# A layer-input gate from seven products of half blocks, and one joint decode series for gate and up

## The chip, the cores and the metric

The kernel runs on one core of a Trainium2 chip. The metric is the time of one execution on the device, in microseconds (us). Five engines work beside each other, each through its own queue in order: TensorE (PE; its weight loads are shown as PEld), VectorE (DVE), ScalarE (ACT), GpSimd (POOL) and SyncE (SP), which here issues the DMAs. SBUF is the working memory, PSUM holds what TensorE writes.

## The reference

One layer of a streaming encoder: 1024 prompt tokens and 8 x 16 new ("decode") tokens, width 1024, all in float32.

```python
x = x + mix @ w_out                      # attention, not touched here
h = rmsnorm(x, g_ffn)
x = x + (jax.nn.silu(h @ w_gate) * (h @ w_up)) @ w_down     # width 2816
gate = jax.nn.sigmoid(rmsnorm(x, g_ple) @ w_ple_gate)       # 1024 x 1024
x = x + gate * (p @ w_ple_proj)
y = rmsnorm(x, g_final)
```

The tokens make nine tiles of 128 rows: prompt tiles 0 to 7 and the decode tile, number 8 (`NP`).

## The kernel before, in words

Every float32 matrix product is made of three products of rounded parts: an operand is split into `hi` (ScalarE's copy, rounded) and `lo` (the rest, a subtraction by `sub`, line 110), and `mm3` (lines 105 to 108) adds hi x hi, hi x lo and lo x hi in one PSUM bank. `Chunks` (line 125) holds the weights: `raw` loads 1 MB into the only buffer `wraw`, `parts` splits it into a pair of tiles `whi`, `wlo`, of which there are two pairs in turn. A pair comes from `pair` (line 138), which takes two tiles of a rotating tag.

The order of the work is set by a planner, which puts each engine's instructions in order by its own idea of their durations, the program's order deciding between those that are ready. Inside `manual_schedule` blocks the named engines keep the program's order.

*The gate and up projections (loop at line 1144).* Chunk i of 22 holds 256 columns of `w_gate` (even i) or `w_up` (odd i). For the 1024 prompt tokens a chunk's product is made by seven products of half blocks in place of eight (`product`, line 1052: 12 matmuls of 512 columns each, recorded at line 1056): B11, B21, T1 to T4 and B22 are forms of the tokens, quarters of the chunk's weights and their sums S1, S2, S0, S3 are the other side. `sums` (line 1074) makes the weights' sums on VectorE, `sum_parts` (line 1084) splits them on ScalarE and GpSimd, `gate_up_parts` splits the next chunk's weights. `first` makes the first product and copies it from its bank to `u2`, after which the second product is added in the same bank. The 128 decode tokens take the plain way: `decoded` (line 1060), a series of 24 matmuls of 256 columns in each chunk, into bank `e`; a gate chunk's `e` goes through the sigmoid to `dec8` (lines 1169 to 1172), an up chunk's is multiplied onto it. At the end of an up chunk `turned` transposes `dec8` and sends the activations to memory.

*The down projection (loop at line 1335).* Five stages d of 512 of the 2816 rows, again by seven products (`times`, recorded at line 1307; `onto`, line 1312, adds a bank to the residual `x1`; `forms`, line 1275, splits the forms). What all the tokens' first quarter has in common with others is kept in `u2`, four tiles. A last step, `down` (line 1409), does the remaining 256 rows plainly, tile by tile: per tile and half of the columns six matmuls of 512 columns, and, for 12 of the 16 prompt halves, the addition of `u2` on GpSimd (line 1414).

*The layer-input gate (line 1425 to the end).* Behind each tile's last step, `normed` scales its row by the root mean square and by the row `g_ple` (line 199), eight transposes (line 1452) and splits make its transposed parts `hV`. `gate(c, w, t)` (line 1428) makes 256 of the 1024 columns for one tile: 24 matmuls of 256 columns, sigmoid (line 1436), times `proj` (line 1437, loaded by the piece), added to `x1` (line 1438, GpSimd, VectorE for the last c), squared with its sum (line 1439). Four c by nine tiles. The final normalization follows in pieces (lines 1474 to 1483).

## Time and profile before

| | |
|---|---|
| runs | 1726.93, 1732.53, 1733.93 us; median 1732.53 |
| profiled execution | 1727.71 us, its span 1725.6 |
| granted TensorE clock, mean | 0.995 |
| DMA, whole span | 279.40 MB, mean 162 GB/s |
| the gate and up loop | about 880 to 1345 us of the span |
| the down stages | about 1345 to 1580 |
| last step of down, transposes, layer-input gate | about 1573 to 1717.8 |

The profile is of one execution. Times in it count from the start of the span. A busy time is the union of an engine's instructions; matmuls overlap one another, so that a busy TensorE says that it has work, not how fast. An idle time is put down to the last of the semaphores for which the instruction waited. "L1056" is line 1056 of the kernel.

### The profile page before, as it was taken

To read this page: it belongs to the slowest core of one execution; us is meant where nothing else is said; L and a number is where in the kernel's file an instruction comes from. 1 tells how busy PE (TensorE), PEld (TensorE's weight loads), DVE (VectorE), ACT (ScalarE), POOL (GpSimd) and SP (SyncE) were. 2 spreads that over 40 slices of the span, in tenths; PEclk is the share of its full clock that TensorE was granted. 3 is DMA by queue.
4 is the path that set the end of the run, shared out by engine and by line. 5 is a ranking of instruction groups with operands and counts; after the bars stand their busy time and mean duration, and the time that the engine had idled before them with its cause. 6 is when DMAs were issued, how large, how long until landed. Compare 5 with 4: busy or idle time off the path is not lost.

```text
span 1725.6 us, 29066 instructions
## 1 busy us (share of the span) xinstructions
PE 1668.2 (97%) x11076; PEld 1457.6 (84%) x11076; DVE 1044.9 (61%) x1640; ACT 776.4 (45%) x1698; POOL 774.3 (45%) x584
## 2 busy tenths in 40 slices
PE   8999999999997998899999999999999999999998
PEld 7998888889995887787778888888888788887998
DVE  5112344277778675654886666666666698887635
ACT  5214545276767776643643333333332343333432
POOL 2313301287446422222455555555554565558364
PEclk9999999999999999999999999999999999999999
DMA  5847898656469986855413222222222874311123
GB/s 191 278 145 226 287 293 284 189 171 184 119 176 267 296 252 185 232 165 176 142 56 115 88 87 90 95 95 95 95 95 95 291 292 136 120 39 61 59 71 141
DMA packets 172620, 279.40 MB, mean 162 GB/s; under 512 B 15297, under 2 KB 103617, under 8 KB 171074
## 3 DMA queue, kind: packets, MB, share of 16 engines
q1 hardware_dynamic: 172482, 277.55, 49.9%
q8 instruction: 88, 1.44, 0.4%
q14 instruction: 50, 0.41, 0.1%
HBM read 197.95 MB, written 79.56 MB: 161 GB/s over the span
## 4 chain that ended last, share of the span: by engine, by line
PE 86%; DMA 5%; DVE 3%; ACT 2%; issue 1%; POOL 1%; SPq 0%; POOLq 0%; ACTq 0%; DVEq 0%
PE ps L1056 20%; PE ps L106 9%; PE ps L107 9%; PE ps L108 9%; PE pt L1307 6%; PE ps L1307 4%; PE pt L1056 3%; PE pt L608 3%; PE pt L395 2%; PE po L632 2%; DMA mixn<-mixp 2%; PE acc L463 2%; PE po L631 2%; PE S L575 1%; PE sdec L418 1%; PE S L576 1%
## 5 line engine op out<-in xcount | busy, mean ns | idle before, releaser
L111 POOL TENSOR_TENSOR wlo<-wraw,whi 128x512 fp32r<-128x512 f32 (+1 forms) x127 | 224.4, 1794 | 205.6 <-ACT whi L150 201.7
L106 PE MATMUL ps<-whi,hTh 128*128 128x256 f32 x576 | 167.7, 291 | 0.1
L107 PE MATMUL ps<-wlo,hTh 128*128 128x256 f32 x576 | 164.2, 285 | 0.0
L108 PE MATMUL ps<-whi,hTl 128*128 128x256 f32 x576 | 163.9, 285 | 0.0
L150 ACT CAST whi<-wraw 128x512 fp32r<-128x512 f32 (+1 forms) x128 | 88.2, 753 | 94.1 <-PE ps L1056 64.8
L589 DVE TENSOR_TENSOR_SCAN keep<-keep,zero 128x128 f32<-128x128 f32 (+4 forms) x64 | 99.1, 1558 | 37.6 <-ACT keep L581 36.6
L590 POOL TENSOR_TENSOR w<-w,keep 128x127 f32<-128x127 f32 (+4 forms) x64 | 83.4, 1313 | 73.1 <-DVE keep L589 64.0
L106 PEld LDWEIGHTS ps<-whi,hTh 128*128 128x128 f32 x576 | 110.2, 191 | 6.0 <-issue 5.4
L108 PEld LDWEIGHTS ps<-whi,hTl 128*128 128x128 f32 x576 | 110.2, 191 | 0.5 <-DVE hTl L111 0.2
L107 PEld LDWEIGHTS ps<-wlo,hTh 128*128 128x128 f32 x576 | 110.3, 192 | 0.1
L111 DVE TENSOR_TENSOR wtl<-pt,wth 128x512 fp32r<-128x512 f32 (+1 forms) x192 | 94.2, 514 | 18.1 <-ACT wth L612 17.2
L612 ACT CAST wth<-pt 128x512 fp32r<-128x512 f32 (+1 forms) x192 | 84.4, 463 | 44.2 <-PE pt L608 43.4
L608 PE MATMUL pt<-ident,w 128*128 128x128 f32 x528 | 87.9, 278 | 5.5 <-POOL w L590 2.1
L106 PE MATMUL ps<-whi,hVh 128*128 128x256 f32 x288 | 81.9, 284 | 0.5 <-ACT hVh L1454 0.5
L107 PE MATMUL ps<-wlo,hVh 128*128 128x256 f32 x288 | 81.7, 284 | 0.0
L108 PE MATMUL ps<-whi,hVl 128*128 128x256 f32 x288 | 81.6, 284 | 0.0
L575 PE MATMUL S<-qk 128*128 128x384 f32 (+2 forms) x192 | 71.4, 373 | 5.8 <-ACT keep L581 3.9
L631 PE MATMUL po<-wth,vk 128*128 128x256 f32 (+1 forms) x304 | 76.3, 283 | 0.2
L608 PEld LDWEIGHTS pt<-ident,w 128*128 128x128 f32 x528 | 61.8, 141 | 15.4 <-issue 3.6
L632 PE MATMUL po<-wtl,vk 128*128 128x256 f32 (+1 forms) x304 | 72.7, 282 | 0.0
L111 POOL TENSOR_TENSOR actl<-actr,acth 128x1024 fp32r<-128x1024 f32 (+1 forms) x22 | 56.7, 2579 | 33.6 <-DMA sr<-acts 18.2
L106 PE MATMUL ps<-hTh,whi 128*128 128x384 f32 x192 | 66.0, 344 | 0.0
(359 smaller groups left out, 5335.9 us busy)
## 6 DMA issues: line engine op xcount, KB each, us to landing
draw<-in_cache_sb_k SPq DMA_DIRECT2D x32, 512.0 KB, 5.3
draw<-in_cache_sb_v SPq DMA_DIRECT2D x32, 512.0 KB, 5.1
act<-sg SPq DMA_DIRECT2D x11, 1152.0 KB
actr<-act SPq DMA_DIRECT2D x22, 576.0 KB, 5.4
wraw<-in_w_in SPq DMA_DIRECT2D x11, 1024.0 KB, 5.2
wraw<-in_w_gate SPq DMA_DIRECT2D x11, 1024.0 KB
wraw<-in_w_up SPq DMA_DIRECT2D x11, 1024.0 KB
v<-sv SPq DMA_DIRECT2D x36, 256.0 KB, 4.5
```

What stands on the lines that cost most here:

```text
L106: T.matmul(out, lhsT=ah, rhs=bh, start=start, stop=False)
L107: T.matmul(out, lhsT=ah, rhs=bl, start=False, stop=False)
L108: T.matmul(out, lhsT=al, rhs=bh, start=False, stop=stop)
L111: eng.tensor_tensor(out, a, hi.bitcast(F32), op=ALU.subtract)
L150: A.copy(h[:, o], v[:, o])
L575: T.matmul(sc, lhsT=hd["qq"][:, qs], rhs=hd["kkh"][:, kc], start=True, stop=False)
L589: V.tensor_tensor_scan(rev, rev, zero[:, 0:1].to_broadcast([P, n]), 1.0, op0=ALU.mult, op1=ALU.add)
L608: T.transpose(pt[:, (c - c0) * P : (c - c0 + 1) * P], w[:, c * P : (c + 1) * P], ident)
L631: T.matmul(dst, lhsT=vs, rhs=wth[:, kb - base, c0:c1], start=(i == 0), stop=False)
L632: T.matmul(dst, lhsT=vs, rhs=wtl[:, kb - base, c0:c1], start=False, stop=(i == nkb - 1))
L1056: T.matmul(out, lhsT=a[x][:, k], rhs=b[y][:, k], start=(not more and k == 0 and n == 0), stop=(k == 3 and n == 2), skip_group_check=more)
L1307: T.matmul(out, lhsT=a[i][:, x, m * P : (m + 1) * P], rhs=b[j][:, x], start=(not more and x == 0 and n == 0), stop=(x == 1 and n == 2), sk ...
```

## The change

Two parts, and what they need.

*The layer-input gate.* Prompt tiles p and p + 4 make a pair, p from 0 to 3. Of their transposed normalized rows, A11 and A12 are tile p's two halves of the 1024 inputs, A21 and A22 tile p + 4's. With S1 = A21 + A22, S2 = S1 - A11, S3 = A11 - A21, S4 = A12 - S2 and four forms of the weights, seven products of 12 matmuls of 512 columns give both tiles' 1024 columns. The weights' forms are B11, B21, T2 = B22 - (B12 - B11), T3 = B22 - B12, T1 = B12 - B11, B21 - T2 and B22; `g_ple` is multiplied onto the weights' rows, no longer onto the tokens. They are made in `gate_sums(k)` during down stages 1 to 4 (four scalings on ScalarE, four operations on GpSimd, four loads and seven stores of 256 KB each) and stored in `gated`; when the down stages' buffers are free, six are loaded back as 1 MB each into `W` and the seventh, B22, into `wraw`. `weights_parts` splits them: W0, W2, W4 and W6 on ScalarE and VectorE, W1, W3, W5 on ScalarE and GpSimd. The decode tile's outputs are sums over B11 and B21 (24 matmuls of 512 columns) and, for the right half, over B11, T1 and B22 (twice 36 of 256).

The `x1 += u2` additions on GpSimd move ahead of the last down step, whose tiles now go in the order 0, 4, 1, 5, 2, 6, 3, 7, 8. From there on TensorE keeps the program's order. Pair p + 1 is prepared (squares, scaling, transposes, sums, splits) between the products of pair p, and pair 0 in the last down step.

*The decode tokens of gate and up.* The two pairs of weight parts become two places of one `hi` and one `lo` tile, so that one matmul can read both: chunks 0 and 1 keep their own series; from then on a gate chunk has none, and the up chunk behind it makes one series of 24 matmuls of 512 columns for both. `issue_after` puts the splits of the next chunk's weights, on ScalarE and GpSimd, behind the split of the last chunk's sum S0. In the qkv projection one line sets which place is next, since places no longer rotate by themselves.

The diff, cut to its core:

```diff
         def pair(self, k, n):
-            out = []
-            for part in ("hi", "lo"):
-                t_ = self.pool.tile([P, self.width], F32R, name=self.pre + part, tag=self.pre + part, bufs=self.pairs)
-                out.append(t_[:, : k * n].rearrange("p (k n) -> p k n", k=k))
-            return out
+            if self.both is None:
+                self.both = [self.pool.tile([P, self.pairs, self.width], F32R, name=self.pre + part) for part in ("hi", "lo")]
+            self.turn = (self.turn + 1) % self.pairs
+            return [t_[:, self.turn, : k * n].rearrange("p (k n) -> p k n", k=k) for t_ in self.both]
...
             if i:
                 a, u2 = first(w)
+            if i == 1:
                 e = decoded(w, tbank(256))
+            elif up:
+                wts, place = ch.pairs_of(KT)
+                both = tbank().rearrange("p (s n) -> p s n", s=2)
+                for k in range(KT):
+                    mm3(both, h8[0][:, k], h8[1][:, k], wts[0][:, :, k], wts[1][:, :, k], k == 0, k == KT - 1)
+                e0, e = both[:, 1 - place], both[:, place]
             if more and i:
                 raw = gate_up(i + 1)
-                nxt = gate_up_parts(raw)
+                with tc.issue_after(made[0]), tc.issue_after(made[1]):
+                    nxt = gate_up_parts(raw)
...
-            if not up:
+            if i == 0 or up and i > 1:
+                g8 = e if i == 0 else e0
                 t8 = p4b.tile([P, 256], F32, name="t8", tag="t8", bufs=1)
-                A.activation(t8, e, AF.Sigmoid)
-                V.tensor_tensor(dec8, t8, e, op=ALU.mult)
-            else:
+                A.activation(t8, g8, AF.Sigmoid)
+                V.tensor_tensor(dec8, t8, g8, op=ALU.mult)
+            if up:
                 V.tensor_tensor(dec8, dec8, e, op=ALU.mult)
...
+    def gate_sums(k):
+        q = {}
+        for x in range(2):
+            for y in range(2):
+                q[x, y] = wq.tile([P, 512], F32, name=f"q{x}{y}", tag=f"q{x}{y}", bufs=1)
+                row = (x * 4 + k) * P
+                nc.sync.dma_start(q[x, y], w_ple_gate[0, row : row + P, y * 512 : y * 512 + 512])
+                A.activation(q[x, y], q[x, y], AF.Copy, scale=g_gate[:, x * 4 + k : x * 4 + k + 1])
...
+        G.tensor_tensor(t3, q[1, 1], q[0, 1], op=ALU.subtract)
+        G.tensor_tensor(q[0, 1], q[0, 1], q[0, 0], op=ALU.subtract)
+        G.tensor_tensor(t2, q[1, 1], q[0, 1], op=ALU.subtract)
+        G.tensor_tensor(q[1, 0], q[1, 0], t2, op=ALU.subtract)
...
+    W = [own_place(i) for i in range(5)] + [ch.pair(4, 512)]
+    for i in range(6):
+        nc.sync.dma_start(W[i][1].bitcast(F32), gated[i])
+    b22 = ch.raw(gated[6], 4, 512)
...
+    final.enter_context(tc.manual_schedule(engines={mybir.EngineType.PE}))
+    weights_parts(0, V)
+    weights_parts(2, V)
+    for i, t in enumerate(tiles):
+        down(t, w_d, act)
+        if i == 1:
+            coming = prepare(0)
+            next(coming)
+            with tc.issue_after(pows[0].ins):
+                weights_parts(1, G)
+        if i == 4:
+            next(coming)
+            weights_parts(3, G)
+            weights_parts(5, G)
+        if i == 6:
+            forms_ = next(coming)
+            with tc.issue_after(last_split[0]):
+                weights_parts(4, V)
+    W.append(ch.parts(b22, 4, 512, 2, V))
+    fetch_proj((0, 4))
+
+    for p in range(4):
+        A11, A12, S2, S3, S1, A22, S4 = forms_
+        u, u3, u4 = u2[3 * (p % 2)], u2[1], u2[2]
+        if p < 3:
+            coming = prepare(p + 1)
+            next(coming)
...
+        a = bank()
+        product(a, A11, W[0])
+        A.copy(u, a)
+        b = bank()
+        product(b, S2, W[2])
+        V.tensor_tensor(u, u, b, op=ALU.add)
+        product(a, A12, W[1], True)
+        c = bank()
+        product(c, S3, W[3])
+        V.tensor_tensor(u3, u, c, op=ALU.add)
+        if p < 3:
+            next(coming)
...
+        with tc.issue_after(last_split[0]):
+            gate(p, 0, 512, 0, a, G)
+        d = bank()
+        product(d, S1, W[4])
+        V.tensor_tensor(u3, u3, d, op=ALU.add)
+        gate(p + 4, 512, 512, 1, u3, G)
+        if p < 3:
+            forms_ = next(coming)
+        product(c, A22, W[5], True)
+        V.tensor_tensor(u4, u, c, op=ALU.add)
+        gate(p + 4, 0, 512, 0, u4, G)
+        close(p + 4, 2)
+        product(d, S4, W[6], True)
+        V.tensor_tensor(u, u, d, op=ALU.add)
+        gate(p, 512, 512, 1, u, G)
+        close(p, 2)
+        fetch_proj((p + 1, p + 5) if p < 3 else (NP,))
```

In `prepare`, the first `next` scales tile p's row, the second makes its eight transposes and the splits of A11 and A12 and scales tile p + 4's row (the row tile `hrow` has one buffer), the third makes the other transposes, the four sums and the five splits. The new `gate` works on 512 (for the decode tile 512 and twice 256) columns; `close` makes the final normalization of one tile in one operation over 1024 columns and sends it out. `proj` comes in 1 MB pieces, one pair of tiles at a time, into `wraw`.

More of the change, by code (lines that the diff above doesn't have):

```diff
@@ L1186, in tile_hymba_step @@
                 S_next = {x: sum_parts(x, s) for x in (1, 2, 0)}
+                made = [m.ins for m in marks]
             product(d, S[3], B22, True)
@@ new lines, in tile_hymba_step, with weights_parts @@
+    tiles = [0, 4, 1, 5, 2, 6, 3, 7, 8]
+    for t in tiles[:-1]:
+        for half in range(2):
+            if t > 3 or half:
+                o = slice(half * 512, half * 512 + 512)
+                G.tensor_tensor(x1[t][:, o], x1[t][:, o], u2[t % 4], op=ALU.add)
+    bstack.close()
+    wf = pool(ctx, "wf", "left")
+    def weights_parts(i, eng):
+        hi, lo = W[i]
+        raw_ = lo.bitcast(F32)
+        for o in (slice(0, 2), slice(2, 4)):
+            A.copy(hi[:, o], raw_[:, o])
+            sub(eng, lo[:, o], raw_[:, o], hi[:, o])
@@ new lines, in scaled, with turned_tile @@
+    def scaled(t, r):
+        h = p6.tile([P, D], F32, name="hrow", tag="hrow", bufs=1)
+        if t % 4:
+            A.activation(h, x1[t], AF.Copy, scale=r[:, 0:1])
+        else:
+            V.tensor_scalar(h, x1[t], r[:, 0:1], None, op0=ALU.mult)
+        return h
+    pows, last_split = [], []
+    def turned_tile(h):
+        pt = [four(tbank()) for _ in range(2)]
+        for i in range(2):
+            for j in range(4):
+                T.transpose(pt[i][:, j], h[:, (i * 4 + j) * P : (i * 4 + j + 1) * P], ident)
+        return pt
@@ new lines, in tile_hymba_step @@
+    h8 = [[v[:, i * 4 : i * 4 + 4] for v in last8] for i in range(2)]
+    for i, (lo, n) in enumerate(((0, 512), (512, 256), (768, 256))):
+        out = bank(n)
+        cut = slice(lo % 512, lo % 512 + n)
+        terms = ((0, 0), (1, 1)) if lo == 0 else ((0, 0), (0, 4), (1, 6))
+        for j, (half, f) in enumerate(terms):
+            for k in range(4):
+                mm3(out, h8[half][0][:, k], h8[half][1][:, k], W[f][0][:, k, cut], W[f][1][:, k, cut],
+                    j == 0 and k == 0, j == len(terms) - 1 and k == 3)
+        gate(NP, lo, n, i, out, V)
@@ L1486 @@
+    close(NP, 3)
 INPUTS = (
```

181 lines of the change are left out of this document (109 added, 72 removed).

## The prediction

> **What bounds the kernel now.** I read the page's engine table first, then the busy times by stretch, the chain that ended last, and last the groups by shape.
>
> ```profile
> span 1725.6 us, 29066 instructions
> PE 1668.2 (97%) x11076; PEld 1457.6 (84%) x11076; DVE 1044.9 (61%) x1640; ACT 776.4 (45%) x1698; POOL 774.3 (45%) x584
> 1012.00:1056.00 44.00, 44.00 (x219) 37.36 (x218) 26.83 (x33) 13.47 (x24) 23.10 (x16) 1.00 0.27 93
> 1480.00:1524.00 44.00, 44.00 (x196) 36.44 (x195) 35.59 (x41) 16.18 (x20) 24.19 (x12) 1.00 0.23 76
> 1524.00:1572.00 48.00, 48.00 (x213) 39.75 (x212) 40.03 (x44) 17.16 (x17) 32.15 (x15) 1.00 0.10 33
> 1572.00:1592.80 20.80, 18.74 (x86) 15.70 (x85) 15.19 (x22) 5.96 (x9) 17.01 (x13) 0.94 0.16 51
> 1637.00:1717.80 80.80, 80.72 (x672) 80.51 (x672) 34.96 (x78) 28.19 (x88) 45.61 (x41) 1.00 0.30 104
> 1717.80:1725.60 7.80, 0.00 (x0) 0.00 (x0) 2.72 (x7) 0.89 (x3) 1.06 (x2) 0.64 0.44 174
> ```
>
> The columns are length, then PE, PEld, DVE, ACT, POOL busy, granted clock, DMA share, GB/s. TensorE is full in one pair of the gate/up loop (1012 to 1056), in the down-projection stages (1480 to 1572) and in the layer-input gate (1637 to 1717.8). So time is taken out only by taking matmuls out, and it is lost again wherever another engine makes TensorE wait. VectorE has 8.4 us of 44 free in a down stage and over half free in the gate of before.
>
> A busy matmul is no price, since matmuls overlap. The price is the distance from start to start:
>
> ```profile
> 1659.72 0.28 PE L107 MATMUL ps<-wlo,hVh 128*128 128x256 f32 x1
> 1671.24 0.28 PE L107 MATMUL ps<-wlo,hVh 128*128 128x256 f32 x1
> 903.96 13.60 PE ps L1056 x60
> ```
>
> Between the first two rows lie 96 matmuls of 256 columns: 11.52 / 96 = 0.120 us each. The third row is the chain's: 60 matmuls of 512 columns in 13.60 us, 0.2267 us each. So 512 columns cost 1.89 times what 256 cost, not twice.
>
> **Term 1, the gate's products.**
>
> ```profile
> L106 PE MATMUL ps<-whi,hVh 128*128 128x256 f32 x288 | 81.9, 284 | 0.5 <-ACT hVh L1454 0.5
> L106 PE MATMUL pt<-whi,h8h 128*128 128x256 f32 x168 | 47.4, 282 | 0.0
> 1572.00:1717.60 145.60, 10.57 (x72) 9.21 (x72) 0.99 0.23 78
> ```
>
> The first row is one of three equal ones (lines 106 to 108): 864 matmuls of 256, 864 x 0.120 = 103.7 us. After, four pairs of prompt tiles take seven products of 12 matmuls of 512 columns each: 336 x 0.2267 = 76.2. The decode tile takes 24 of 512 and, since B12 is not among the forms, three half-products for each of two 256-column outputs, 72 of 256: 5.4 + 8.6 = 14.1. Together 90.2: **-13.4 us**. The 108 matmuls of the last down step and the 72 transposes (10.57 us in the third row, 0.147 each) stay.
>
> **Term 2, the joint decode series.** The second row stands for 504 matmuls, and 24 more lie in the first chunk. Chunks 0 and 1 keep theirs. The other 480 x 0.120 = 57.6 become 240 x 0.2267 = 54.4: **-3.2 us**. The gate chunk's place is now read until the up chunk's joint series ends; by the count of products that is 24 matmuls (5.4 us) and one product ahead of them (2.7) later than now.
>
> ```profile
> 1024.43 2.19 ACT L150 CAST whi<-wraw 128x512 fp32r<-128x512 f32 x4 [2.38 <-PE ps L1056]
> 1025.13 5.51 POOL L111 TENSOR_TENSOR wlo<-wraw,whi 128x512 fp32r<-128x512 f32 x4 [3.19 <-ACT whi L150]
> 1041.64 0.39 PE L1056 MATMUL ps<-B11h,whi 128*128 128x512 f32 x1
> PE ps L1056 <- DVE u L1182: 0.5, 1, 0.5
> ```
>
> The rewriting takes 6.2 us (1024.43 to 1030.64) and its first reader starts at 1041.64: 11 us of slack, of which the later start takes some 8. It holds, so I put it at nothing. If it did not, some us would show in each of ten pairs. Putting the sums' parts first removes no wait: in the whole loop TensorE's longest sum of waits is 0.5 us (last row).
>
> **Term 3, the waits of this stretch that go.**
>
> ```profile
> PE pt L1452 <- DVE hrow L199: 2.1, 1, 2.1
> PE ps L106 <- ACT hVh L1454: 0.5, 1, 0.5
> ```
>
> Both belong to the old transposes: **-2.6 us**, and what is late instead is the next term.
>
> **Term 4, the new waits.** Three places.
>
> First, the end of the down stages. TensorE there fills a wait for VectorE (two halves of a weight split, 4.62 us) with matmuls of the last step:
>
> ```profile
> 1568.73 4.62 DVE L111 TENSOR_TENSOR wlo<-wr,whi 128x1024 fp32r<-128x1024 f32 x2
> 1573.59 0.39 PE L107 MATMUL ps<-wlo,acth 128*128 128x512 f32 x1
> 1576.09 0.39 PE L1307 MATMUL pt<-whi,acth 128*128 128x512 f32 x1
> ```
>
> From 1573.59 to 1576.09 eleven of them run. After, the last step's TensorE order is written out behind the stages, so this 2.5 us is bare. Bounds 0 and 2.5; the split is unchanged, so I take **+2.5**.
>
> Second, VectorE while the weights' forms are split.
>
> ```profile
> L1418 DVE TENSOR_TENSOR x<-x,ps 128x512 f32<-128x512 f32 x18 | 12.2, 684 | 5.1 <-PE ps L108 5.0
> L111 DVE TENSOR_TENSOR wlo<-t,whi 128x1024 fp32r<-128x1024 f32 x15 | 25.6, 1726 | 3.5 <-ACT whi L1266 3.5
> L111 DVE TENSOR_TENSOR wlo<-wraw,whi 128x1024 fp32r<-128x1024 f32 x5 | 11.4, 2276 | 0.9 <-ACT whi L1266 0.9
> L1209 DVE TENSOR_TENSOR su<-su,sg 128x512 f32<-128x512 f32 x10 | 6.8, 678 | 0.0
> L1132 DVE TENSOR_TENSOR sg<-sg,u 128x512 f32<-128x512 f32 x30 | 49.8, 1660 | 1.0
> L199 DVE SCALAR_TENSOR_TENSOR hrow<-x,r_n,row_grow 128x1024 f32<-128x1024 f32 x9 | 12.4, 1384 | 0.9 <-POOL r_n L117 0.9
> L1482 DVE TENSOR_SCALAR x<-x,r 128x1024 f32<-128x1024 f32 x9 | 6.7, 748 | 0.6 <-POOL r L1480 0.4
> L1474 DVE TENSOR_REDUCE part<-ss 128x1 f32<-128x3 f32 x9 | 1.4, 155 | 4.7 <-ACT sgp L1439 4.7
> ```
>
> One 128x512 operation takes 0.68 us with an operand in PSUM or with GpSimd quiet (684, 678 ns) and up to 1.66 with both operands in SBUF (1660). During the last step VectorE has 18 additions (12.3), four halves of W0 and W2 (4 x 1.73 to 2.28 = 6.9 to 9.1), and pair 0's forms: seven operations from PSUM, one split in SBUF, two scalings of 0.75 and small ones, 8 us. That is 27 to 29.5 us against TensorE's 108 x 0.2267 + 16 x 0.147 = 26.8. In a pair it has 12 operations from PSUM (8.2), five in SBUF (3.4 to 8.3), two closings (2.8 to 4.6) and 8 small ones (1.2): 15.6 to 22.3, middle 19, against 84 x 0.2267 + 2.35 = 21.4. Pair 0 also bears W4 and W6, four halves, 6.9 to 9.1: 26 to 28 against 21.4. So VectorE falls 5 to 9 us behind by the end of pair 0. TensorE bears a lag of 12 matmuls and 16 transposes (5.1 us) between the product that fills a bank and the one that adds to it. The difference is 0 to 4; the wait can come at the upper end since operations also stand in the queue behind others. I take **+4** (bounds 0 and 8).
>
> Third, the middle of pairs 0 to 2: the second transposes need the second tile's row, which is scaled after the first transposes have read the only buffer. ScalarE must in 2.72 us (one product) copy two halves and scale 1024 columns:
>
> ```profile
> L150 ACT CAST whi<-wraw 128x1024 fp32r<-128x1024 f32 x8 | 8.2, 1045 | 13.7 <-PE pt L1307 11.4 <-PE ps L108 2.3
> L1071 ACT COPY u<-ps 128x512 f32<-128x512 f32 x21 | 12.2, 581 | 0.0
> L1414 POOL TENSOR_TENSOR x<-x,v 128x512 f32<-128x512 f32 x12 | 19.0, 1621 | 0.0
> wraw<-in_w_out SPq DMA_DIRECT2D x4, 1024.0 KB, 5.4
> 1579.94 0.39 PE L1307 MATMUL pt<-whi,actl 128*128 128x512 f32 x1
> ```
>
> 2 x 0.58 + 1.05 = 2.2 and the hand-overs: just met or just missed, 0 to 1.5 us each; I take 0.8, so **+2.5** (bounds 0 and 4.5).
>
> ScalarE in a pair: seven splits, two copies, four sigmoids and eight squares (21 x 0.58), two scalings (2.1) and the reading of eight sums: about 16 of 21.4. GpSimd: three splits and four additions (7 x 1.62 = 11.3) and four one-column powers: about 14. Neither binds.
>
> **What costs nothing.** The sums of the gate's weights, made in stages 1 to 4: four GpSimd operations (6.5 us) and four ScalarE scalings (2.4) each, where GpSimd has 20 us and ScalarE 28 us of 44 free (row 1480). Behind them on SyncE's queue stand seven stores of 256 KB and the next stage's loads; those are asked for a stage (44 us) ahead and a 1 MB load lands in 5.4 us (fourth row), at a DMA share of 0.23. Bounds 0 and 1 us a stage, through VectorE's slower operations; I take 0. The twelve GpSimd additions (19 us) only move. The forms, six loads of 1 MB, wait for the down stage's buffers. VectorE leaves the last of those at 1573.3 (row 1568.73). Six times 5.4 from there, even end to end, is 1605.7. The stages' last matmul starts at 1579.94 (row above), and with the last step's 26.8 behind it the pairs start near 1607; W0, the first in the queue, lands by 1579 and W5 is read only in the sixth product. If that cover went, each 1 MB is 5.4 us of waiting. SyncE also waits with the next pair's 1 MB of proj until the last multiplication of the pair before; only the sigmoid's product waits for it, not a bank.
>
> **The end.** The tail from the last matmul (7.8 us, row 1717.8) grows by a closing operation of 1.38 in place of 0.75, and one small one: **+0.8**.
>
> **The sum.** -13.4 - 3.2 - 2.6 + 2.5 + 4 + 2.5 + 0.8 = -9.4. The profiled execution took 1727.71 us (span 1725.6), so 1718.3 on its footing. The three other times are 1726.93, 1732.53 and 1733.93; the middle of all four is 1730.1, 2.4 above it. Forecast: 1720.7.
>
> **What a page would make of it.** The Trainium skill, "TensorE: Matmul & The Clock Gate", the part on the clock gate ("Wait — 56ns, not 53.3ns?"), gives a warm matmul N / 2.4 GHz + 2.5 ns: an estimate of 0.109 for 256 and 0.216 for 512 columns. By it terms 1 and 2 would be 8.8 and 0.6, and the sum -2.2. The trace differs (0.120 and 0.2267), and it measured both forms in this kernel. "SBUF — State Buffer", on the shared port pair, says that a VectorE operation with two SBUF inputs and a GpSimd operation that reads SBUF shut each other out for a whole instruction. The trace agrees with its direction (678 against 1660 ns); it speaks against this change, and the third rival carries it.
>
> **The rivals.**
>
> 1. VectorE keeps up (0.20). For: 18% of it is free even in a down stage, and its low durations give 15.6 of 21.4 a pair. Then only the bare 2.5 us stays: 1730.1 - 15.9 = 1714.
>
> 2. The wait eats the gain (0.25). The second and third places of term 4 at their upper ends (8 and 4.5) and 1 us in each of four stages: 1730.1 + 0.6 = about 1729; part of it, 1724 to 1729.
>
> 3. On the other side, slower (0.10): VectorE becomes the bound from the last down step to the end. Place: the two-SBUF operations, beside a GpSimd that is busy two thirds of the time. All of them at 1.66 and 2.28: 29.5 + 3 x 22.3 + 15.7 (the last pair, which prepares no other) + 9.1 = 121 us against TensorE's 26.8 + 3 x 21.4 + 20.2 = 111. As the bound in order it would also stand idle between TensorE's products, a tenth to a fifth (it is idle 19% in row 1480): 134 to 149, so +23 to +38 in place of +6.5, and 1737 to 1752. It decides from where a pair's VectorE work passes 21.4, that is with most of the five at 1.6. Against: row 1480 shows that VectorE need not be slow throughout beside a GpSimd busy for more than half of the time.
>
> 4. In the gate chunks no decode series stands any more between the first product and its continuation on the same bank, which must wait for ScalarE's copy (0.08). For: the one place where that is bare cost 1.8 us:
>
> ```profile
> PE ps L1056 <- ACT u L1071: 1.8, 1, 1.8
> 1030.73 0.40 PE L1056 MATMUL pt<-T2h,S1h 128*128 128x512 f32 x1
> ```
>
> Ten times 0.6 to 1.8 gives +6 to +18, about 1732. Against: the second row, where T2's product starts before B21's, so the planner has other work to put there.
>
> 5. The longer matmuls do not bring their price: 512 columns cost twice 256, so that 256 at 0.1133 had been hidden behind something else (0.02). Then term 1 is 864 - 792 halves of 0.1133 = 8.2, term 2 nothing, and the time 1729. Against: both distances above, from unbroken stretches. The page's formula goes this way. Or the joined tiles make writes of one place wait for readers of the other (0.01); some 6 us in each of 20 chunks, over 1800.
>
> **How the numbers follow.** The forecast has 0.34. A measurement of this kernel can tell about 0.5% (8.7 us) from no change. The forecast lies 9.4 below like for like, so three quarters of its chance count as faster: 0.26, with rival 1 at 0.20 and the better part of rival 2, 0.04: 0.50. Slower: rival 3 and the worst of 4 and 5: 0.12. The rest, 0.38, is the same. The range goes from every new wait at zero on the fastest footing (1726.9 - 18.4 = 1709) to the point where rivals 2 and 4 end (1735), leaving out most of rivals 3 and 5.
>
> **What would show it.** Right: 336 + 24 matmuls of 512 columns and 72 of 256 in the gate, a gate that starts near 1604, pairs of 21.5 to 23 us; ten joint series at 0.227 us a matmul, each pair of gate and up chunks 0.3 shorter; TensorE waits of 6 to 12 us between 1565 and the end, for VectorE first. Wrong: VectorE over 20 us busy in a pair with TensorE under 9 tenths; waits of "ps" for ScalarE's u in the gate chunks; or loads of the forms that release TensorE.

## The result and the profile after

| | before | after |
|---|---|---|
| median, us | 1732.53 (5 runs, 1726.93 to 1733.93) | 1718.60 (5 runs, 1716.57 to 1721.59) |
| profiled execution, us | 1727.71 | 1716.96 |
| span, us | 1725.6 | 1715.2 |
| granted clock, mean | 0.995 | 0.992 |

The ratio is 0.9929, with a 95% interval from 0.9915 to 0.9943: 12.3 us faster on 1732.5, where 11.8 stood between the forecast of 1720.7 and that median. Like for like the sum had said 9.4. The total was nearly right. Its terms were not, and errors of both signs cancelled.

The page's first lines, after:

```profile
span 1715.2 us, 27832 instructions
PE 1656.5 (97%) x10404; PEld 1421.2 (83%) x10404; DVE 1071.8 (62%) x1646; ACT 809.9 (47%) x1713; POOL 809.9 (47%) x590
```

TensorE lost 672 instructions and 11.7 us of busy time; its share of the span is what it was. Now the busy times by stretch, after: three of the four pairs of the new gate, and the tail (columns as before: length, PE, PEld, DVE, ACT, POOL, clock, DMA share, GB/s).

```profile
1604.00:1625.50 21.50, 21.33 (x104) 17.90 (x105) 19.39 (x26) 9.63 (x14) 15.71 (x9) 1.00 0.13 50
1625.50:1647.00 21.50, 21.50 (x107) 18.08 (x106) 16.46 (x28) 14.92 (x32) 12.97 (x12) 1.00 0.27 99
1647.00:1668.00 21.00, 21.00 (x102) 17.55 (x101) 15.99 (x27) 14.62 (x33) 12.46 (x11) 1.00 0.27 101
...
1707.00:1715.20 8.20, 0.27 (x3) 0.06 (x1) 2.44 (x5) 0.90 (x3) 0.55 (x1) 0.72 0.16 64
```

TensorE is full in these pairs, with VectorE at 19.4 us of 21.5 in pair 0 and about 16 in the others. TensorE's whole list of waits from 1575 to 1715 us, after, has one row:

```profile
PE pt L1519 <- DVE hrow L1510: 0.7, 1, 0.7
```

Nine us of new waits had been forecast for that stretch. The chain that ended last, after, in its last part, says the same in TensorE's own terms (start, length, what):

```profile
1625.25 0.87 PE pt L1519 x8
1626.12 16.35 PE ps L1064 x72
...
1643.34 2.75 PE ps L1064 x12
...
1646.96 16.35 PE ps L1064 x72
```

Between the two long rows lie 20.84 us, one pair. 72 matmuls in 16.35 are 0.2271 each, the price that the forecast took from the old loop. The joint series in the loop, after, has it too (the first two of 24 rows of one matmul):

```profile
1033.14 0.23 PE pt L106
1033.37 0.23 PE pt L107
```

To see where the rest went, cut the span at four points: the first and the last T2 product of the loop, and the first and the last product of the decode tokens in the down stages (`d8h`). The single-tile view gives them as "first to last start". Before:

```profile
L1056 PE MATMUL pt<-T2h,S1h x88: 389/389/397, 877.5 to 1344.5; 128*128 128x512 f32 x88
L106 PE MATMUL ps<-whi,d8h x40: 389/389/389, 1368.2 to 1566.1; 128*128 128x512 f32 x40
```

After:

```profile
L1064 PE MATMUL pt<-T2h,S1h x88: 389/389/503, 885.0 to 1349.6; 128*128 128x512 f32 x88
L106 PE MATMUL ps<-whi,d8h x40: 389/389/389, 1373.4 to 1574.8; 128*128 128x512 f32 x40
```

| stretch | before | after | difference | forecast |
|---|---|---|---|---|
| start to the first T2 product ("the front") | 877.5 | 885.0 | +7.5 | 0 |
| the loop, first to last T2 | 467.0 | 464.6 | -2.4 | -3.2 |
| last T2 to first d8h | 23.7 | 23.8 | +0.1 | 0 |
| the stages, first to last d8h | 197.9 | 201.4 | +3.5 | 0 |
| last d8h to the end | 159.5 | 140.4 | -19.1 | -6.2 (terms 1, 3, 4, tail) |
| sum | 1725.6 | 1715.2 | -10.4 | -9.4 |

The forecast failed in the first, the fourth and the fifth row, by +7.5, +3.5 and -12.9. Of the fourth row 2.0 us are no cost: after, 874 matmuls and not 865 lie between the first and the last d8h product, so nine matmuls (9 x 0.227) have only moved out of the last row. All experiments below are read by this table.

### The profile page after: what moved, and what is told of

The parts are those of the page before. It is cut to its first block, busy times and chain, and to the rows that moved or that the text cites. A ratio compares the mean times of both kernels' runs of the same rounds, so it can differ in the third digit from the quotient of the medians.

```text
span 1715.2 us, 27832 instructions
## 1 busy us (share of the span) xinstructions
PE 1656.5 (97%) x10404; PEld 1421.2 (83%) x10404; DVE 1071.8 (62%) x1646; ACT 809.9 (47%) x1713; POOL 809.9 (47%) x590
## 4 chain that ended last, share of the span: by engine, by line
PE 81%; DVE 5%; DMA 5%; ACT 4%; issue 2%; POOL 2%; SPq 0%; POOLq 0%; ACTq 0%; DVEq 0%
PE ps L1064 24%; PE ps L106 7%; PE ps L107 7%; PE ps L108 7%; PE pt L1327 4%; PE pt L1064 3%; PE ps L1327 3%; PE pt L616 3%; PE pt L403 3%; PE po L640 2%; PE po L639 2%; PE S L583 2%; PE acc L471 2%; PE sdec L426 1%; DMA v<-sv 1%
## 5 line engine op out<-in xcount | busy, mean ns | idle before, releaser
L111 POOL TENSOR_TENSOR wlo<-wraw,whi 128x512 fp32r<-128x512 f32 (+1 forms) x119 | 212.4, 1809 | 139.6 <-ACT whi L155 139.6
L597 DVE TENSOR_TENSOR_SCAN keep<-keep,zero 128x128 f32<-128x128 f32 (+4 forms) x64 | 102.1, 1604 | 32.6 <-ACT keep L589 32.2
L111 POOL TENSOR_TENSOR actl<-actr,acth 128x1024 fp32r<-128x1024 f32 (+1 forms) x22 | 61.5, 2795 | 32.4 <-DMA sr<-acts 20.7
L404 DVE COPY kT<-pt 128x512 f32<-128x512 f32 x48 | 33.0, 688 | 52.8 <-PE pt L403 48.8
L107 PE MATMUL ps<-hTl,whi 128*128 128x384 f32 x192 | 65.6, 342 | 0.0
L108 PE MATMUL ps<-hTh,wlo 128*128 128x384 f32 x192 | 65.2, 339 | 0.0
```

The costliest lines, as they stand in the source:

```text
L107: T.matmul(out, lhsT=ah, rhs=bl, start=False, stop=False)
L108: T.matmul(out, lhsT=al, rhs=bh, start=False, stop=stop)
L111: return eng.tensor_tensor(out, a, hi.bitcast(F32), op=ALU.subtract)
L597: V.tensor_tensor_scan(rev, rev, zero[:, 0:1].to_broadcast([P, n]), 1.0, op0=ALU.mult, op1=ALU.add)
```

## The experiments

Every ratio is to the kernel before, measured beside it on the same chip (its medians there: 1732.11 us for e1 to e4, 1731.39 for e5 to e8, 1731.66 for e9 to e12). Theory A, from the two traces: the gate brings about 15 us, the loop 2.5, and the joined places cost several us ahead of the loop. Rival B: the front's +7.5 is the chance of one execution, and the gate brings only the difference.

**e1, the joined places alone** (old gate, old series, no order):

```diff
         def pair(self, k, n):
-            out = []
...
-            return out
+            if self.both is None:
+                self.both = [self.pool.tile([P, self.pairs, self.width], F32R, name=self.pre + part) for part in ("hi", "lo")]
+            self.turn = (self.turn + 1) % self.pairs
+            return [t_[:, self.turn, : k * n].rearrange("p (k n) -> p k n", k=k) for t_ in self.both]
...
+                ch.turn = 1 - ch.turn
                 load(i + 2)
```

> Only the two pairs of weight parts become places of one tile; no joint series, the old gate. Main theory (the change lost about 8 us ahead of the gate and up loop, because the joined places alter the order in which the planner puts the qkv and attention stages): slower than before by 5 to 9 us, with the out-projection's first upper-half product (hU) near 722 us where before has 715, and more TensorE time at half clock ahead of 880 us. Rival (those 8 us are the chance of one profiled execution): within 2 us of before.

Measured: 1745.82 us, ratio 1.0088 (1.0073 to 1.0103), 13.7 slower, above what either theory expected. The out-projection's first hU product starts at 722.7, as the main theory had it. Most of the loss lies in the loop:

```profile
L1063 PE MATMUL pt<-T2h,S1h x88: 389/389/494, 886.0 to 1364.7; 128*128 128x512 f32 x88
```

478.7 us against 467.0. The chain of waits between 1050 and 1100 us, which in the kernel before is all TensorE, runs in e1 through the one weight buffer instead:

```profile
1049.53 5.22 DMA wraw<-in_w_up
...
1064.07 1.71 DVE s L1085
...
1070.41 0.61 DVE s L1088
1071.04 5.49 DMA wraw<-in_w_gate
...
1094.20 5.51 DMA wraw<-in_w_up
```

From load to load 21.5 and 23.2 us. GpSimd's own rows (the bracket is the idle time ahead and its releaser) show how the ring closes. Before, its chunk has the parts of S1, S2 and S0, then the next weights' splits:

```profile
1058.86 1.29 POOL L111 TENSOR_TENSOR S1l<-s,S1h 128x512 fp32r<-128x512 f32 x1 [3.66 <-ACT S1h L1086]
...
1064.31 1.52 POOL L111 TENSOR_TENSOR S0l<-s,S0h 128x512 fp32r<-128x512 f32 x1 [1.43 <-ACT S0h L1086]
1069.27 5.51 POOL L111 TENSOR_TENSOR wlo<-wraw,whi 128x512 fp32r<-128x512 f32 x4 [3.44 <-ACT whi L150]
```

In e1 two of the four splits stand ahead of S1's part:

```profile
1055.52 2.54 POOL L111 TENSOR_TENSOR wlo<-wraw,whi 128x512 fp32r<-128x512 f32 x2 [7.53 <-ACT whi L155]
1058.02 1.28 POOL L111 TENSOR_TENSOR S1l<-s,S1h 128x512 fp32r<-128x512 f32 x1
```

GpSimd sits idle for 7.5 us until the next chunk's load has landed and is split, and only then makes the part of the present chunk's sum. So a chunk's sums wait for the next load, and the next load but one waits until VectorE has read `wraw` for its sums. The likely reason, not tried by itself: joined places are freed piece by piece, so that in the planner's eyes some splits can start sooner, and it sets them first. TensorE's waits are short (3.9 us for `u` in three pieces, one of 3.6), but the loop runs at this ring's pace.

**e2, the new gate alone** (rotating pairs, old series):

```diff
-            if self.both is None:
-                self.both = [self.pool.tile([P, self.pairs, self.width], F32R, name=self.pre + part) for part in ("hi", "lo")]
...
+            out = []
+            for part in ("hi", "lo"):
...
-            if i == 1:
                 e = decoded(w, tbank(256))
-            elif up:
```

> Only the new layer-input gate; rotating pairs and a decode series in each chunk as before. Main theory: the front part is as before, and the stretch from the down stages' end gives its full 16 to 17 us: 14 to 17 us faster than before, so 2 to 5 us faster than the whole change. Rival (chance, not the places): the whole change less its joint series, so 3 us slower than the whole change, 8 to 10 us faster than before.

Measured: 1722.09 us, ratio 0.9943 (0.9927 to 0.9958), 10.0 faster, as the rival's 8 to 10 had it; the main theory's 14 to 17 failed. Its last stretch does bring what theory A says (144.2 us, 15.3 under before), but its down stages take 204.7 us, 6.8 more than before, with three waits of TensorE, of which before has only one of the second kind:

```profile
PE pt L1311 <- ACT whi L1270: 1.9, 1, 1.9
PE ps L1311 <- DVE x L1316: 1.6, 1, 1.6
PE pt L1311 <- DVE wlo L111: 1.5, 1, 1.5
```

A stretch of half clock follows there too: the granted clock is 0.50 from 1488 to 1492, right behind the first and the third of these waits (they end at 1486.4 and 1488.4), and these two waits with the slow matmuls behind them make up the 6.8. And its order of instructions ahead of the stages is that of the kernel before, on every engine, yet its loop starts at 881.6, not 877.5: some 4 us of the front's +7.5 are within the chance of one execution, as rival B says.

**e3, the decode part alone** (e1 with the joint series and the order):

```diff
-                e = decoded(w, tbank(256))
+            if i == 1:
+                e = decoded(w, tbank(256))
+            elif up:
+                wts, place = ch.pairs_of(KT)
...
-                nxt = gate_up_parts(raw)
+                with tc.issue_after(made[0]), tc.issue_after(made[1]):
+                    nxt = gate_up_parts(raw)
```

> Only the decode part: joined places, joint series, sums' parts first; the old gate. Main theory: the loss of the places less 3.2 to 3.5 us of the series: 2 to 6 us slower than before, and 3 us faster than the places alone. Rival (the front is chance): 3 us faster than before. In the trace both expect a pair of gate and up chunks of 43.7 to 43.9 us in place of 44.1.

Measured: 1731.83 us, ratio 1.0002 (0.9993 to 1.0011), no difference; the main theory's 2 to 6 slower and the rival's 3 faster both missed. Its loop takes 464.5 us, -2.5 as forecast; it starts at 886.6. What the loop gains, the front takes. Its stages and last stretch, with the old gate, are 199.7 and 155.8 us. In sum that is 1.9 less than before's 197.9 + 159.5, about what one stretch of half clock cost there (1.7, below): with joined places the nine matmuls named above stand ahead of the last `d8h` product. Against 155.8 the new gate's 140.4 is 15.4 less.

**e4, the whole change without the order:**

```diff
-                with tc.issue_after(made[0]), tc.issue_after(made[1]):
-                    nxt = gate_up_parts(raw)
+                nxt = gate_up_parts(raw)
```

> The whole change without the order that puts the sums' parts first. If that order matters, the next weights' splits get in ahead of the sums' and TensorE waits for S0 or S1 once in each chunk, 0.3 to 1.5 us each: 5 to 20 us slower than the whole change. My prediction counted it at nothing: then within 1.5 us of the whole change.

Measured: 1723.73 us, ratio 0.9952 (0.9937 to 0.9966), 8.4 faster, some 4 less than the whole, so between the two forecasts (within 1.5, or 5 to 20 slower). Its loop takes 466.5, with TensorE waiting 1.7 us for VectorE's `u`. So the order has a worth, of which the loop shows 2 us, and the joint series alone undoes most of e1's loss in the loop.

**e5, the whole change again**, beside e6, e7 and e8.

> The whole change again, on the chip of the three runs beside it. 11 to 13 us faster than before. If the gate's 10.0 and the decode part's 0.3 simply add up, 10.3; more would say that the parts help each other.

Measured: 1719.11 us, ratio 0.9928 (0.9914 to 0.9942), 12.3 faster. That is 2.0 more than the parts' 10.0 and 0.3 together, but the intervals of e2 and e5 reach some 2.5 us to either side, so that the parts help each other isn't shown.

**e6, without the sums of the gate's weights.** It leaves the forms and the scaling by `g_ple` out and loads the places of the forms from `x1d` instead, so that the loads stay and the work of `gate_sums` goes. `g_gate` stays, as a tile among the constants with one small operation on ScalarE:

```diff
-        if d:
-            gate_sums(d - 1)
...
-        nc.sync.dma_start(W[i][1].bitcast(F32), gated[i])
-    b22 = ch.raw(gated[6], 4, 512)
+        nc.sync.dma_start(W[i][1].bitcast(F32), block(i))
+    b22 = ch.raw(block(6), 4, 512)
```

> The whole change without the sums of the gate's weights in the down stages: the six forms and B22 are loaded from blocks of another array of the same size, so the forms and their scaling are left out. My prediction counted the sums at nothing: within 1.5 us of the whole change. Rival (they slow VectorE's two-input operations in the stages and TensorE waits for it): 2 to 5 us faster than the whole change, and the joint tile d8h's products from first to last in 198 to 200 us, as where the old gate stands, in place of 201.4.

Measured: 1718.87 us, ratio 0.9921 (0.9906 to 0.9937), the same as the whole. That looks like "the sums cost nothing", and the stretches say otherwise:

```profile
L1064 PE MATMUL pt<-T2h,S1h x88: 389/394/499, 881.8 to 1352.9; 128*128 128x512 f32 x88
L106 PE MATMUL ps<-whi,d8h x40: 389/389/389, 1376.9 to 1576.6; 128*128 128x512 f32 x40
```

The stages take 199.7 us, as in all three other kernels with joined places and no sums (e1, e3, e11: 199.7 each), where the eight kernels with joined places and the sums take 201.4 to 202.8: the sums cost 1.7 to 3.1 us. The total hides it, since e6's loop takes 471.1 us, 6.5 more, with TensorE's order unchanged. The median duration in the first row is 394 ns, not 389, and e6's chain shows the price:

```profile
1309.33 13.84 PE ps L1064 x60
1323.17 2.80 PE pt L1064 x12
1325.97 8.33 PE ps L1064 x36
```

36 matmuls took 8.16 us in the whole change and take 8.33 here, at the same granted clock. This is told further below.

**e7, more on VectorE:** three splits and four additions of each pair move from GpSimd to VectorE (seven lines like these):

```diff
-        split(v, G)
-        split(s1, G)
+        split(v, V)
+        split(s1, V)
...
-            gate(p, 0, 512, 0, a, G)
+            gate(p, 0, 512, 0, a, V)
```

> The whole change with the three GpSimd splits and the four GpSimd additions of each pair on VectorE: some 5 us more of VectorE in a pair of 21 us. If VectorE had only a little room, as my prediction had it (19 of 21.4, and behind by 5 to 9 us at the end of pair 0), TensorE waits for it in each pair: 5 to 15 us slower. If it had the 5 us that the profile after shows (16 to 17 of 21), and its operations get shorter beside an idle GpSimd: within 2 us of the whole change.

Measured: 1718.63 us, ratio 0.9924 (0.9908 to 0.9941), the same as the whole. Busy time of pair 1, e7:

```profile
1625.50:1647.00 21.50, 21.50 (x105) 17.91 (x104) 18.91 (x36) 14.30 (x31) 2.13 (x4) 1.00 0.27 99
```

VectorE got seven more operations and is 2.4 us busier, at 18.9 of 21.5; TensorE is full. From 1575 us on TensorE has one wait here, of 0.6 us for `hrow`, as in the whole change. The prediction had 19 a pair for the change itself.

**e8, the whole change with the old rotation ahead of the loop.** A pair is one tile of a rotating tag until just before the loop, and two joined places from there:

```diff
+        def place(self, name):
+            return self.pool.tile([P, 2, self.width], F32R, name=self.pre + name, tag=self.pre + "pair", bufs=2)
+        def join(self):
+            self.both = [self.place(part) for part in ("hi", "lo")]
...
             if self.both is None:
-                self.both = [self.pool.tile([P, self.pairs, self.width], F32R, name=self.pre + part) for part in ("hi", "lo")]
+                t_ = self.place("pair")
+                return [t_[:, x, : k * n].rearrange("p (k n) -> p k n", k=k) for x in range(2)]
...
-                ch.turn = 1 - ch.turn
...
+    ch.join()
```

> The whole change, but the weight parts rotate tile by tile (hi and lo of a pair in one tile) until the last output weights, and become places only there. If the joined places cost the front part 4 us: 3 to 5 us faster than the whole change, with the first hU product near 718 us. Rival (the front part's length hangs on its exact order and on which waits drop TensorE's clock, not on the places): anything within 4 us either way, since this order is a third one.

Measured: 1713.28 us, ratio 0.9896 (0.9877 to 0.9915), 18.1 faster than before and 5.8 faster than e5 beside it, a little above the 3 to 5 forecast. Its first hU product starts at 716.8 and the loop at 881.0.

**e12, e8 once more,** since one arrangement with one profile is little evidence.

> The whole change with the weight parts rotating tile by tile until just before the gate and up loop, and joined places only from there, once more (it took 1713.28 us, 18.1 less than the kernel before). Theory (joined places cost 4 to 6 us ahead of the loop): 16 to 20 less than the kernel before again, 1711 to 1716. Rival (that run was one lucky arrangement or the chance of the clock): 11 to 15 less, as the whole change.

Measured: 1715.08 us, ratio 0.9908 (0.9891 to 0.9924), 16.6 faster. It begins the loop at 883.5. The two ratios lie 0.2 to 0.3% under the whole's two (0.9929 and 0.9928). This is the fastest version found, faster than both kernels.

**e9, e8 with e7's seven lines.**

> The same front, and three splits and four additions of each pair on VectorE in place of GpSimd. By itself that move changed nothing (18.6 against 18.7 and 19.1). Theory (VectorE has room, TensorE is bare nowhere): within 2 us of the kernel with the same front alone. Rival (GpSimd's port sharing still costs something at the end): 2 to 4 us less.

Measured: 1716.49 us, ratio 0.9915 (0.9900 to 0.9930), 1.4 from e12. VectorE has room here too, and nothing is gained.

**e10, e8 without the order** (e4's lines).

> The same front, without the two waits that put the sums' parts first. Theory (the order is worth its 4 us inside the loop, whatever the front is, since joined places free their parts piecewise there): 3 to 6 us slower than with the order, with TensorE waits for VectorE's u in the loop. Rival (the order's worth was in the front): no difference.

Measured: 1718.32 us, ratio 0.9926 (0.9910 to 0.9941), 3.2 slower than e12, with intervals that overlap. Its loop takes 465.6 us, 1.0 to 2.0 more than with the order (464.6 in e8, 463.6 in e12), with 1.3 us of waits for `u`. With e4 this makes two pairs that agree on 3 to 5 us in all. The loop shows 1 to 2 of them; where the others lie isn't settled.

**e11, the decode part alone (e3) with e8's front.**

> The decode part alone (old layer-input gate), with the tile by tile front and joined places only from the loop on. With joined places from the start it gained 0.3 us. Theory (the loop gives 2.5 and the front of joined places takes about as much or more): 2 to 7 us less than the kernel before. Rival (the loss lies in the decode part itself): within 1 us of the kernel before.

Measured: 1729.94 us, ratio 0.9992 (0.9979 to 1.0005), 1.7 faster, the theory's 2 to 7 just missed and the rival's 1 as well. Up to 1471 us its TensorE order is e8's, but it starts its loop at 886.6.

**The front, from all profiles.** One order doesn't start the loop at one time. Before's order: 877.5 and 881.6. Joined places from the start (after, e1, e3, e4, e5, e6, e7): 881.8 to 888.9, mean 886.2. e8's order (e8 to e12): 881.0 to 886.6, mean 883.8. So by the profiles the joined places cost about 2 us against e8's front and 6 or 7 against before's, with some 2 us of chance in each. By the ratios five pairs of kernels differ in this front alone: e8 and e5 (5.5 us), e12 and the first runs of the whole (3.6), e9 and e7 (1.6), e10 and e4 (4.5), e11 and e3 (1.7). The change of front wins in all five, 3.4 us in the mean. Theory A holds for the front, with a smaller size than the two first profiles showed; rival B holds for the rest of the +7.5.

The trace's record of the granted clock says where the difference lies. Ahead of the loop before has 6.8 us at half clock, e2 with the same order 23.9, e8 to e12 17.1 to 27.3, and the kernels with joined places from the start 23.9 (after) to 34.1. An estimate: half of that time is what the slow clock can cost. Taken off each front, it leaves 869 to 875 us in 13 of the 14 profiles, whatever the arrangement (e6: 865). So an arrangement seems to count by the waits that it brings and the slow clock behind them, as e8's rival had it. These are three orders of one program; that joined places cost something as such isn't shown.

What such a front loses can be seen at the wait for `mixn`, 75 us ahead of the loop. TensorE's rows after, at the longest such wait but one:

```profile
806.25 0.39 PE L108 MATMUL ps<-whi,hUl 128*128 128x512 f32 x1
810.41 1.51 PE L910 MATMUL pt<-ident,mixn 128*128 128x128 f32 x6 [3.77 <-DMA mixn<-mixp]
...
812.54 0.63 PE L107 MATMUL ps<-wlo,hUh 128*128 128x512 f32 x1
812.97 0.63 PE L106 MATMUL ps<-whi,hUh 128*128 128x512 f32 x1
```

The wait takes 3.77 us, and behind it 512-column matmuls start every 0.43 us, not every 0.227. Over the whole front the waits for `mixn` are (sum, times, longest), after and then before:

```profile
PE pt L910 <- DMA mixn<-mixp: 10.8, 3, 4.5
```

```profile
PE pt L902 <- DMA mixn<-mixp: 7.7, 4, 2.8
```

What delays that transfer in one arrangement and not in another wasn't tried.

## Why the prediction was right or wrong

*Term 1, the gate's products: right.* The price per matmul (0.2271) and the pairs' 84 stand in the chain. Against e3, which has the old gate behind the same loop, the last stretch is 15.4 us shorter; -13.4 - 2.6 + 0.8 = -15.2 had been the sum without new waits. The 72 transposes stayed as they were, 9.39 us busy after and 9.43 in e3; the 10.57 of before held a slow clock, next point. The tail did not grow by 0.8: from the end of the last matmul to the end of the span both traces have 7.9 us.

*Term 3, the old waits: right in place; in before's execution more hung on them.* The page's row for the wait (2.1 us) wasn't its whole price there. Before, in two stretches of 3 us just behind it:

```profile
1591.00:1594.00 3.00, 3.00 (x15) 2.93 (x14) 1.88 (x5) 2.79 (x7) 0.52 (x1) 0.55 0.48 167
1594.00:1597.00 3.00, 3.00 (x17) 2.58 (x16) 3.00 (x6) 1.17 (x3) 0.58 (x2) 1.00 0.00 0
```

The third number from the end is the clock: 0.55, then 1.00. Some 3.4 us at half clock followed the wait, 1.7 us lost. In a page's row of 80 us this is rounded away, and the row 1572 to 1592.8 quoted in the prediction had shown 0.94 without its being priced. It is no fixed part of the wait: e1, e3 and e11 keep the old gate and have the same wait (2.0 us), and the clock stays at 1.00 behind it in e1 and e3 and falls for 3.4 us in e11. Their last stretches take 155.8, 155.8 and 157.1 us.

*Term 4, the new waits: failed, +9.0 against 0.7.* Three steps of it:

First, "this 2.5 us is bare": it wasn't. TensorE's rows after, while the last splits of the stages were made:

```profile
1579.33 0.39 PE L106 MATMUL ps<-whi,acth 128*128 128x512 f32 x1
...
1581.60 0.39 PE L107 MATMUL ps<-wlo,acth 128*128 128x512 f32 x1
...
1583.86 0.39 PE L108 MATMUL ps<-whi,actl 128*128 128x512 f32 x1
1584.09 0.39 PE L1327 MATMUL pt<-whi,acth 128*128 128x512 f32 x1
```

Fifteen matmuls of the last step (lines 106 to 108: four from 1579.33, eleven from 1581.60) still run ahead of the stages' last products (line 1327). A written order holds within its block; it doesn't keep the block's first instructions from being put among those of the code ahead of it. That TensorE can wait for such a split is seen in e2, where 1.5 us for `wlo` show at 1488, in an earlier stage.

Second, VectorE 5 to 9 us behind by the end of pair 0: it never was. VectorE's groups after, 1604 to 1700 us (count, busy us, mean ns):

```profile
L1581 DVE TENSOR_TENSOR sgp<-sgp,pj 128x512 f32<-128x512 f32 x17 | 14.2, 836 | 3.3 <-ACT sgp L1580 3.3
L1533 DVE TENSOR_TENSOR actl<-s,acth 128x512 fp32r<-128x512 f32 x4 | 5.0, 1258 | 0.0
L111 DVE TENSOR_TENSOR wlo<-wraw,whi 128x1024 fp32r<-128x1024 f32 x2 | 4.5, 2306 | 0.0
```

The weights' splits cost what was forecast (this one at its upper end). The five operations a pair with both operands in SBUF were put in the middle of 0.68 and 1.66; four of the five took 0.84 on the mean, the fifth 1.26. A row's scaling, put at 0.75, took 1.63 (L1510 in the same view), without a wait in the pairs. Pair 0's stretch has VectorE at 19.4 of 21.5 us, where the forecast had 26 to 28; the others have it at 16 to 17. Rival 1 (VectorE keeps up) is what happened in the gate. e7 showed how far it was from the limit: with seven more operations a pair, still no new wait.

Third, ScalarE made the second row in time: 2.75 us of products stand between the two sets of transposes in the chain above, with no wait for `hrow` there. The one of 0.7 us stands at 1604 in the last down step, where VectorE scales the second row of pair 0.

*The sums, at nothing: too low.* They cost 1.7 to 3.1 us, within the stated bounds of 0 to 1 a stage, in the stages and not in the gate.

*Term 2, the joint series: right.* Of nine profiles with series and order eight have loops of 463.6 to 464.6 us (the ninth is e6, with 471.1 for the reason told below); two with the old series and rotating tiles (before and e2) have 467.0 and 468.3.

*"Putting the sums' parts first removes no wait": failed.* It removes none that the kernel before had. It holds off what joined places bring: in e1, without the joint series, the ring from load to load by way of splits set ahead of the sums' parts (11.7 us in the loop), and with the joint series, in e4 and e10, 1 to 2 us of the loop. The forecast asked of the joined places only whether a place is read too late; whether they let other work ahead was not asked. The row it rests on (11 us of slack) held: TensorE has no wait for `whi` or `wlo` in the loop after.

*The front, at nothing: failed.* `pair` serves every weight of the kernel, and joined places changed the order of the work far ahead of the loop: TensorE's order differs from 315 us on, ScalarE's from 75. The prediction priced the helper only where the diff uses it anew.

*The rivals and the signs.* Besides rival 1 and what rival 2 had for the sums, none is seen. Rival 4's wait of TensorE for ScalarE's `u` shows once before and once after, 1.8 us each, ahead of the loop and not in the gate chunks. Rival 5's doubled price isn't there: 0.2271 per matmul stands in the new gate. No load of the forms released TensorE. Rival 2's upper end should have read 1730.7 (1730.1 + 0.6), not 1729.

*The footing.* The profiled execution of before was near the fast end: four of its five first runs took 1731.65 to 1733.93, and its medians beside the experiments are 1731.4 to 1732.1. From there the change brings 12 to 14 us. The ledger roughly agrees: of the forecast's 9.4, 0.8 fell out in the loop; the last stretch brought 12.9 more (8.3 of waits that did not come, 2.0 of matmuls moved into the stages, 1.7 of before's slow clock, 0.7 of tail); the stages took 3.5. That would make 18, and the front takes 4.6 to 6.6 of it (the mean of 886.2 against e2's 881.6, or against the mean of 881.6 and 877.5), which leaves 11 to 13. So the total came out near the forecast by luck: 9 us of waits that hardly came were set off by a front and sums that had been put at nothing.

## What to carry to other kernels

A wait's price is the wait and, in some executions, a slow clock behind it, so read the granted clock in stretches as short as 3 us, and do not build a difference on one execution's slow stretch. A change to a helper is a change at each of its callers: cut both spans at a few products that both kernels have, and compare the stretches ahead of the change too, since a total that comes out right may be a sum of errors. When a tile's parts come free sooner, ask which engine's queue the next work enters, and what it gets ahead of.

## What the runs showed of the hardware

*Half clock behind a wait.* The stretches after, around the wait for `mixn` quoted above:

```profile
806.00:809.00 3.00, 0.63 (x3) 0.19 (x1) 0.62 (x1) 0.10 (x1) 2.41 (x4) 1.00 1.04 381
809.00:812.00 3.00, 1.56 (x7) 1.17 (x7) 0.07 (x1) 0.62 (x2) 0.00 (x0) 0.58 0.38 129
812.00:815.00 3.00, 3.00 (x8) 2.34 (x9) 1.17 (x2) 0.54 (x1) 0.00 (x0) 0.50 0.00 0
815.00:818.00 3.00, 3.00 (x15) 2.16 (x14) 1.24 (x2) 1.73 (x3) 0.00 (x0) 0.79 0.00 0
```

By these shares the clock falls some 3 us into the wait and comes back nearly 7 us later, well after TensorE has work again. The trace's record of the clock has these stretches in multiples of 3.41 us. Without the tail, where TensorE has no work, they make 10.2 us in the execution of before, 23.9 in that of after, 17.1 in that of e8; each 3.41 us with work costs 1.7. The Trainium skill, "TensorE: Matmul & The Clock Gate", section "HAM oscillation — how this bites in real kernels", tells of the same: a wait longer than a window of about 3.4 us, then half rate for the work behind it. The trace agrees for the 3.77 us wait. But a wait's length alone does not decide it here: before, 2.1 us of waiting up to 1589.9 had been enough, while the waits of 2.8, 2.4 and 2.1 us for `mixn` before, and that of 2.0 us in e1 and e3, had no slow stretch behind them. The mean granted clock of an execution goes with its time: the five of after lie between 1716.57 us at 0.992 and 1721.59 at 0.986.

*VectorE beside GpSimd.* Two of the three groups above, the first and the third, in e7 over the same 96 us, with GpSimd 18.3 us busy and not 58.3:

```profile
L1581 DVE TENSOR_TENSOR sgp<-sgp,pj 128x512 f32<-128x512 f32 x16 | 11.0, 685 | 1.7 <-ACT sgp L1580 1.7
L111 DVE TENSOR_TENSOR wlo<-wraw,whi 128x1024 fp32r<-128x1024 f32 x2 | 2.4, 1212 | 0.0
```

The mean is 685 against 836 ns, and 1212 against 2306 for the split of 1024, during which GpSimd stands idle in e7. The Trainium skill, "SBUF — State Buffer", section "SBUF: two separate sides", has the two shut each other out for a whole instruction. The trace agrees: the long operation about doubles. The multiplications of the gate met GpSimd seldom: their mean of 836 ns lies nearer to 685 than to the 1660 of the row in the prediction.

*The same matmul at two prices.* In e6's loop the products that read the sums S0 to S3 take 395 ns by the groups, and 36 of them 8.33 us on the chain (0.231 each), against 389 and 8.16 (0.227) in the whole change; other products are unchanged, the granted clock is 1.00 in both, and TensorE's order in the loop is the same. e6 differs ahead of the stages by one small tile, `g_gate` with 32 bytes a partition, which lies among the constants there. That it moved the tiles of the sums to other addresses, and that the address makes the price, is a guess that wasn't tried.
